# Inverse blocks transposed straight from the masked scores, key transposes moved into the inverse, token shift on VectorE, low-rank products on row halves

## The chip, the cores and the metric

One core of a Trainium2 chip runs one program. The metric is the device time of one execution in microseconds. Before: 2159.66 us, the median of three runs (2159.29 to 2162.8).

## The reference, cut to what matters

A sequence of 4096 tokens of width 1024 is normalised and modulated, multiplied with one input matrix, and goes through two branches: a pooling mixer (stage one of the kernel) and an RWKV-7 time mixing with 8 heads of size 64 (stage two). Both outputs are concatenated, multiplied with the output matrix, gated, added to the residual and normalised. The change touches only the RWKV part:

```python
seg = seg + (prev - seg) * mu_shift            # token shift: this row and the row before
r, w_lo, k, v, a_lo, z = jnp.split(seg, split_idx, axis=-1)
w_raw = w0 + jnp.tanh(w_lo) @ w_up             # low-rank decay, rank 64
a = jax.nn.sigmoid(a0 + a_lo @ a_up)           # low-rank rate, rank 64
...
def step(S, inp):                              # one token; S is (H, 64, 64)
    r_t, w_t, k_t, v_t, am_t, b_t = inp        # am = -kk, b = kk * a
    sa = jnp.einsum('bhij,bhj->bhi', S, am_t)
    S = S * w_t[:, :, None, :] + sa[..., None] * b_t[:, :, None, :] + v_t[..., None] * k_t[:, :, None, :]
    return S, jnp.einsum('bhij,bhj->bhi', S, r_t)
```

The kernel computes the recurrence in chunks of 64 tokens. Within a chunk it needs, for each head, the inverse of a 64x64 triangular matrix that is built from products of rates and keys.

## The kernel before, in words

**Stage one** (to about 420 us) normalises and transforms the input, runs the pooling branch, and writes the hidden rows in two float16 parts (hT_hi, hT_lo) to HBM. **Stage two** runs over 16 blocks `b` of 256 tokens (4 chunks, 8 heads, so 32 chunk-heads). In every block four things happen, and the last of them belongs to the next block:

- `scores(b)`: for each chunk the 64-row products of BK (keys) and AR (queries and rates) on TensorE into two PSUM banks (L673), masked by VectorE into `sc` (L680). Then, before, the four 128x128 transposes of this chunk's BK (`btp`, L701), copied by ScalarE to `BT` (L702). BT is first read in `chain` (L851).
- `inverse(b)`: the two 32x32 diagonal blocks of each of the 32 matrices are inverted. Before, ScalarE copies them from `sc` into a corner of `MT` (L719, twice), VectorE transposes the corner to `Ab` (L725) and scales it by `d2T` (L726), ScalarE copies `Ab` to the other 64 partitions (L727) and fills `W` from it (L729, twice). Then a loop of 30 steps, each of two dependent small VectorE operations (L735, L740). Behind it: a scale (L751), two transposes of W into MT (L753), one of MT into `MQ` (L754), a ScalarE copy (L755), and two rounds of 32x32 products (`qp` L764, `m21p` L772) with ScalarE copies between.
- `chain(b)`: the four chunks in turn, each with products that depend on the state S, evicted by ScalarE and VectorE.
- `front(b+1)`: a Python generator with the next block's 17 projections (`seg`, L558 to 571). A projection is 8 triplets of float16 matmuls (L563 to 565) into a PSUM tile with the tag "pj"; the pool has three such buffers, shared with the low-rank products `pl` (L596) and `pa` (L613), with `vps` (L638) and with `pb` (L651). ScalarE reads the tile twice, once for this row (L567) and once for the row before (`prev`, L569), and VectorE adds the two (L570).

The generator yields after every triplet. `fill(n)` advances it by n yields, so the constants FS, FI, FT, FQ, FA, FB, FY say how many triplets TensorE gets between the steps of scores, inverse and chain. In the last block `project` takes the place of the front. A scheduler then orders each engine's instructions; `tc.high_priority` lifts the steps of the inverse over the front's. On every engine instructions run in the order of its queue. In the low-rank products before, `up_w` and `up_a` are padded with zeros to 128 rows, so each product takes all 128 rows of `lo`, whose lower 64 partitions hold the decay's part and whose upper 64 the rate's.

Of the kernel before, what the change touches and what calls it, by code (L numbers as in the profile page):

```python
# [10 lines left out]
F32 = mybir.dt.float32  # L11
# [3 lines left out]
AF = mybir.ActivationFunctionType  # L15
ALU = mybir.AluOpType
# [4 lines left out]
P = 128  # L21
D = 1024
KT = D // P
NPAIR = 4
# [28 lines left out]
def kernel(  # L53
# [19 lines left out]
    TB2 = 256  # L73
    NB2 = T // TB2
    NCH = TB2 // C
    NI = NCH * NH

    FS, FT, FQ, FA, FB, FY = 2, 13, 4, 3, 2, 2
    FI = [5 - i % 2 for i in range(16)]
    PF = 0.6  # L80
    PRI = 400

    V, A, G, PE, SP = nc.vector, nc.scalar, nc.gpsimd, nc.tensor, nc.sync

    cpool = ctx.enter_context(tc.tile_pool(name="cpool", bufs=1))
# [17 lines left out]
    up_w, up_a = (cpool.tile([P, 512], F32, name=n) for n in ("up_w", "up_a"))  # L103
# [35 lines left out]
    with ExitStack() as ph:  # L139
# [313 lines left out]
        def prep_lora():  # L453
            for t_, o in ((up_w, 0), (up_a, 64)):
                G.memset(t_[64 - o : 128 - o], 0.0)
                SP.dma_start(t_[o : o + 64], lora_up[o : o + 64])

        NA = 3
        for b in range(NB1):
# [11 lines left out]
            if b == 0:  # L471
                prep_lora()
# [18 lines left out]
    with ExitStack() as ph:  # L491
# [56 lines left out]
        def front(b, f):  # L548
# [9 lines left out]
            def seg(m, name, bufs=2):  # L558
# [9 lines left out]
                pv_ = wk.tile([P, TB2], F32, tag="prev", name=f"prev{b}_{m}", bufs=2)  # L568
                A.activation(pv_, pp[:, :TB2], AF.Identity, bias=0.0, scale=c2[:, m : m + 1])  # L569
                V.tensor_add(sg, sg, pv_)  # L570
# [15 lines left out]
            for p in range(NPAIR):  # L586
# [7 lines left out]
                pl = ps_pj.tile([P, TB2], F32, tag="pj", name=f"pl{b}_{p}")  # L594
                ps_ = slice(p * P, (p + 1) * P)
                PE.matmul(pl, up_w[:, ps_], lo, start=True, stop=True)  # L596
                tw = wk.tile([P, TB2], F32, tag="tw", name=f"tw{b}_{p}")
                A.activation(tw, pl, AF.Tanh, bias=pv[:, HW0, p : p + 1], scale=0.5)
                A.activation(tw, tw, AF.Identity, bias=one, scale=1.0)
# [12 lines left out]
                pa = ps_pj.tile([P, TB2], F32, tag="pj", name=f"pa{b}_{p}")  # L612
                PE.matmul(pa, up_a[:, ps_], lo, start=True, stop=True)  # L613
                ta = wk.tile([P, TB2], F32, tag="ta", name=f"ta{b}_{p}")
                A.activation(ta, pa, AF.Tanh, bias=pv[:, HA0, p : p + 1], scale=0.5)
# [5 lines left out]
                V.tensor_mul(ta, ta, kS)  # L621
                V.tensor_mul(BK[:, p, :, 1, :], c3(ta), c3(Pi))
                V.tensor_mul(AR[:, p, :, 1, :], c3(rS), Pp[:, :, 1:])
# [36 lines left out]
        def scores(b, f, fill):  # L660
# [6 lines left out]
            for ch in range(NCH):  # L667
# [31 lines left out]
                pt = ps_sc.tile([P, 512], F32, tag="sc", name=f"btp{b}_{ch}")  # L699
                for p in range(NPAIR):  # L700
                    PE.transpose(pt[:, p * P : (p + 1) * P], BK[:, p, ch].rearrange("q a t -> q (a t)"), ident)  # L701
                A.copy(BT[:, ch, :], pt)  # L702
# [5 lines left out]
        def inverse(b, f, fill):  # L708
# [3 lines left out]
            fi = iter(FI)  # L712
            sc, d2T = f["sc"], f["d2T"]
            MT = f["UV"][0:64].rearrange("q c (h t) -> q (c h) t", h=NH)

            with tc.high_priority(offset=PRI):
                for kb in range(2):
                    o = 32 * kb
                    A.copy(MT[o : o + 32, :, 0:32], sc[o : o + 32, :, o : o + 32])  # L719
            fill(next(fi))  # L720
            Ab = blk.tile([P, 32, 32], F32, tag="Ab", name=f"Ab{b}")
            W = blk.tile([P, 16, 32], F32, tag="W", name=f"W{b}")

            with tc.high_priority(offset=PRI):
                V.transpose(Ab[0:64], MT[:, :, 0:32].rearrange("s i t -> s t i"))  # L725
                V.tensor_mul(Ab[0:64], Ab[0:64], d2T[0:64].unsqueeze(2).to_broadcast([64, 32, 32]))  # L726
                A.copy(Ab[64:128], Ab[0:64])  # L727
                for g in range(2):
                    A.copy(W[64 * g : 64 * g + 64], Ab[64 * g : 64 * g + 64].rearrange("q (t g) s -> q t g s", g=2)[:, :, g, :])  # L729
# [331 lines left out]
```

## Time and profile before

| | |
|---|---|
| median of three runs | 2159.66 us |
| the profiled execution's own time | 2165.94 us |
| its span | 2164.2 us |
| PE busy, share of the span | 2002.0 us, 93% |
| DVE busy | 1399.5 us, 65% |
| ACT busy | 1112.2 us, 51% |
| mean granted TensorE clock | 0.966 |

A busy PE in this profile is not a PE at its peak: matmuls are pipelined and their ends are modelled. How fast TensorE goes is read from the distance of the starts of successive matmuls, and where it waits from the idle time in brackets before an instruction. Stage two is periodic, so one block in the middle is read closely (block 8, from 889.74 us, and block 9 behind it, from 976.78 us).

### The profile page before, as it was taken

What the parts mean: (1) busy time and instruction counts of PE and PEld (TensorE: products, weight loads), DVE (VectorE), ACT (ScalarE), POOL (GpSimd) and SP (SyncE); (2) the same over time, 40 slices, a digit from 0 to 9 for tenths busy, and PEclk for the clock granted to TensorE, in tenths of its full rate; (3) what the DMA queues carried; (4) which work ended last, traced back from release to release, by engine and by line L of the source; (5) the groups of instructions that cost most, each with busy time, mean ns of one, the idle gap of its engine ahead of it and who ended that gap; (6) DMA issues with size and microseconds to landing.
All of it is one profiled execution on the core that took longest, in us unless ns stands there. A gap on an engine that the chain in (4) does not pass through costs nothing.

```text
span 2164.2 us, 48675 instructions
## 1 busy us (share of the span) xinstructions
PE 2002.0 (93%) x20186; PEld 1498.8 (69%) x20186; DVE 1399.5 (65%) x3501; ACT 1112.2 (51%) x2455; POOL 150.9 (7%) x272
## 2 busy tenths in 40 slices
PE   4999999998998998999989989999899889999998
PEld 2444444687777777777777777777777767788887
DVE  8798987456756767567566675675766857433433
ACT  2545433356566655666666656665666663321211
POOL 3000000000000000000000000000000000100000
PEclk7999999999999999999999999999999999999999
DMA  7876767200010110101001101011010433444431
GB/s 276 274 236 230 247 216 261 64 21 9 23 32 1 31 27 6 31 2 31 26 7 31 26 6 31 2 31 27 6 31 17 132 105 121 156 156 137 146 107 69
DMA packets 140463, 183.22 MB, mean 85 GB/s; under 512 B 12113, under 2 KB 94033, under 8 KB 140242
## 3 DMA queue, kind: packets, MB, share of 16 engines
q1 hardware_dynamic: 140242, 180.11, 25.4%
q8 instruction: 158, 2.59, 0.5%
q14 instruction: 63, 0.52, 0.1%
HBM read 121.22 MB, written 58.85 MB: 83 GB/s over the span
## 4 chain that ended last, share of the span: by engine, by line
PE 57%; DVE 23%; ACT 14%; issue 3%; DMA 2%; SPq 0%; POOL 0%; DVEq 0%; POOLq 0%; ACTq 0%
PE pj L563 6%; PE po L961 5%; PE po L963 5%; PE po L962 5%; PE pj L565 5%; PE pj L564 5%; PE pp L414 4%; PE pp L416 4%; PE pp L415 4%; DVE W L740 4%; DVE Wt L735 4%; PE scp_sc L673 2%; ACT mx L900 2%; PE psn L851 2%; ACT UV L719 1%
## 5 line engine op out<-in xcount | busy, mean ns | idle before, releaser
L563 PE MATMUL pj<-hh,w2h 128*128 128x257 f16 x2176 | 621.8, 286 | 57.2 <-ACT prev L569 54.7
L565 PE MATMUL pj<-hh,w2l 128*128 128x257 f16 x2176 | 615.3, 283 | 0.0
L564 PE MATMUL pj<-hl,w2h 128*128 128x257 f16 x2176 | 614.4, 282 | 0.0
L564 PEld LDWEIGHTS <-w2h 128*128 128x128 f16 x2176 | 221.5, 102 | 105.5 <-issue 72.2
L563 PEld LDWEIGHTS <-w2h 128*128 128x128 f16 x2176 | 218.9, 101 | 51.6
L565 PEld LDWEIGHTS <-w2l 128*128 128x128 f16 x2176 | 217.8, 100 | 38.4
L961 PE MATMUL po<-wo,mh 128*128 128x512 f32 x512 | 204.7, 400 | 5.5 <-ACT mh L945 5.5
L962 PE MATMUL po<-wo,mh 128*128 128x512 f32 x512 | 202.0, 395 | 0.0
L415 PE MATMUL pp<-lo,w1h 128*128 128x512 f16 x512 | 194.6, 380 | 1.2 <-DVE lo L227 1.2
L416 PE MATMUL pp<-hi,w1l 128*128 128x512 f16 x512 | 194.5, 380 | 0.0
L414 PE MATMUL pp<-hi,w1h 128*128 128x512 f16 x512 | 194.0, 381 | 0.4 <-ACT hi L226 0.2
L967 ACT ACTIVATE sq<-x 128x512 f32<-128x512 f32 x64 | 40.4, 631 | 214.7 <-DVE x L965 199.2
L965 DVE TENSOR_TENSOR x<-po,x 128x512 f32<-128x512 f32 x64 | 44.1, 689 | 156.5 <-PE po L963 156.5
L735 DVE TENSOR_TENSOR Wt<-W,Ab 128x30 f32<-128x30 f32 (+7 forms) x480 | 118.3, 247 | 37.7 <-ACT W L729 27.7
L569 ACT ACTIVATE prev<-pj,c 128x256 f32<-128x256 f32 x272 | 126.9, 467 | 0.0
L740 DVE TENSOR_TENSOR W<-W,Wt 128x30 f32<-128x30 f32 (+7 forms) x480 | 117.9, 246 | 9.1
L961 PEld LDWEIGHTS po<-wo,mh 128*128 128x128 f32 x512 | 96.9, 189 | 27.5 <-ACT mh L945 5.8
L962 PEld LDWEIGHTS po<-wo,mh 128*128 128x128 f32 x512 | 96.9, 189 | 22.2
L963 PE MATMUL po<-wo,ml 128*128 128x512 f32 x256 | 102.0, 399 | 0.0
L416 PEld LDWEIGHTS <-w1l 128*128 128x128 f16 x512 | 50.3, 98 | 61.8 <-issue 2.5
L414 PEld LDWEIGHTS <-w1h 128*128 128x128 f16 x512 | 50.3, 98 | 59.4 <-issue 1.5
L415 PEld LDWEIGHTS <-w1h 128*128 128x128 f16 x512 | 50.2, 98 | 59.2 <-issue 0.6
(248 smaller groups left out, 3850.9 us busy)
## 6 DMA issues: line engine op xcount, KB each, us to landing
x<-in_x_dram SPq DMA_DIRECT2D x64, 256.0 KB, 3.0
out_dram<-x SPq DMA_DIRECT2D x64, 256.0 KB, 2.1
xk<-in_xT_dram SPq DMA_DIRECT2D x56, 256.0 KB, 4.1
xt<-in_x_dram SPq DMA_DIRECT2D x28, 512.0 KB, 5.5
wada<-in_w_ada_dram SPq DMA_DIRECT2D x24, 512.0 KB, 7.0
w2raw<-in_w_in_dram SPq DMA_DIRECT2D x17, 512.0 KB, 5.5
hh<-hT_hi SPq DMA_DIRECT2D x32, 257.0 KB, 3.5
hl<-hT_lo SPq DMA_DIRECT2D x32, 257.0 KB, 3.0
```

Source lines behind the costliest of these rows:

```text
L414: PE.matmul(pp, w1_hi[m][:, k, :], hi, start=(k == 0), stop=False)
L415: PE.matmul(pp, w1_hi[m][:, k, :], lo, start=False, stop=False)
L416: PE.matmul(pp, w1_lo[m][:, k, :], hi, start=False, stop=(k == KT - 1))
L563: unpin(PE.matmul(pp, w2_hi[m][:, k, :], hh[k], start=(k == 0), stop=False))
L564: PE.matmul(pp, w2_hi[m][:, k, :], hl[k], start=False, stop=False)
L565: PE.matmul(pp, w2_lo[m][:, k, :], hh[k], start=False, stop=(k == KT - 1))
L569: A.activation(pv_, pp[:, :TB2], AF.Identity, bias=0.0, scale=c2[:, m : m + 1])
L735: V.tensor_mul(tmp[:, :n, :k], W[:, r0:, k : k + 1].to_broadcast([P, n, k]), Ab[:, k : k + 1, :k].to_broadcast([P, n, k]),)
L740: V.tensor_add(W[:, r0:, :k], W[:, r0:, :k], tmp[:, :n, :k])
L961: unpin(PE.matmul(po, mh[:, k, ts_], wo[0][k][n], start=(k == 0), stop=False))
L962: PE.matmul(po, mh[:, k, ts_], wo[1][k][n], start=False, stop=False)
L963: PE.matmul(po, (ml[:, k] if b % 2 == 0 else ml[k])[:, ts_], wo[0][k][n], start=False, stop=(k == KT - 1))
```

## The change

1. `inverse`: VectorE transposes the diagonal blocks straight from `sc` (two transposes of 32 partitions, L708 of the new file); the two ScalarE copies into MT are gone. W is filled by two VectorE copies (L712) in place of two by ScalarE.
2. The four groups of key transposes (`btp`) and their copies to BT go from `scores` to `inverse`, each followed by `fill(FE)` with FE = 2. FI becomes 4 everywhere (64 yields in place of 72), FT 12 in place of 13.
3. `up_w` and `up_a`, padded, become one tile `up`, loaded at the program's start; `pl` takes partitions 0 to 63, `pa` 64 to 127, and `pa` with its tanh moves up beside `pl`.
4. `seg`: the second ScalarE operation and the addition become one VectorE operation that reads the PSUM tile (L562 of the new file).

```diff
--- before.py
+++ after.py
@@ -75,8 +75,8 @@
     NCH = TB2 // C
     NI = NCH * NH
 
-    FS, FT, FQ, FA, FB, FY = 2, 13, 4, 3, 2, 2
-    FI = [5 - i % 2 for i in range(16)]
+    FS, FE, FT, FQ, FA, FB, FY = 2, 2, 12, 4, 3, 2, 2
+    FI = [4] * 16
     PF = 0.6
     PRI = 400
 
@@ -100,7 +100,8 @@
     SP.dma_start(vec, vecs)
 
 
-    up_w, up_a = (cpool.tile([P, 512], F32, name=n) for n in ("up_w", "up_a"))
+    up = cpool.tile([P, 512], F32, name="up")
+    SP.dma_start(up, lora_up)
 
     def pow2_scale(pool, psp, am, n, name):
 
@@ -450,11 +451,6 @@
             for f in todo[max(b - 1, 0) : b] if b < NB1 - 1 else todo[max(b - 1, 0) :]:
                 f()
 
-        def prep_lora():
-            for t_, o in ((up_w, 0), (up_a, 64)):
-                G.memset(t_[64 - o : 128 - o], 0.0)
-                SP.dma_start(t_[o : o + 64], lora_up[o : o + 64])
-
         NA = 3
         for b in range(NB1):
             if b == 0:
@@ -468,8 +464,6 @@
                 pz, pu = proj(b, hs, (4, 0))
                 pooled(b, 0, pu, gated(b, 0, pz))
             side(b)
-            if b == 0:
-                prep_lora()
             for g in range(1, 4):
                 if b == 0:
                     tz = tzs[g]
@@ -565,9 +559,7 @@
                     PE.matmul(pp, w2_lo[m][:, k, :], hh[k], start=False, stop=(k == KT - 1))
                 sg = wk.tile([P, TB2], F32, tag=name, name=f"{name}{b}_{m}", bufs=bufs)
                 A.activation(sg, pp[:, 1:], AF.Identity, bias=0.0, scale=c1[:, m : m + 1])
-                pv_ = wk.tile([P, TB2], F32, tag="prev", name=f"prev{b}_{m}", bufs=2)
-                A.activation(pv_, pp[:, :TB2], AF.Identity, bias=0.0, scale=c2[:, m : m + 1])
-                V.tensor_add(sg, sg, pv_)
+                V.scalar_tensor_tensor(sg, pp[:, :TB2], c2[:, m : m + 1], sg, op0=ALU.mult, op1=ALU.add)
                 return sg
 
             AR = blk.tile([P, NPAIR, NCH, 2, C], F32, tag="AR", name=f"AR{b}", bufs=2)
@@ -591,11 +583,14 @@
                 yield
                 rS = yield from seg(2 + 4 * p, "rS")
 
-                pl = ps_pj.tile([P, TB2], F32, tag="pj", name=f"pl{b}_{p}")
                 ps_ = slice(p * P, (p + 1) * P)
-                PE.matmul(pl, up_w[:, ps_], lo, start=True, stop=True)
+                pl, pa = (ps_pj.tile([P, TB2], F32, tag="pj", name=f"{n}{b}_{p}") for n in ("pl", "pa"))
+                PE.matmul(pl, up[0:64, ps_], lo[0:64], start=True, stop=True)
+                PE.matmul(pa, up[64:128, ps_], lo[64:128], start=True, stop=True)
                 tw = wk.tile([P, TB2], F32, tag="tw", name=f"tw{b}_{p}")
                 A.activation(tw, pl, AF.Tanh, bias=pv[:, HW0, p : p + 1], scale=0.5)
+                ta = wk.tile([P, TB2], F32, tag="ta", name=f"ta{b}_{p}")
+                A.activation(ta, pa, AF.Tanh, bias=pv[:, HA0, p : p + 1], scale=0.5)
                 A.activation(tw, tw, AF.Identity, bias=one, scale=1.0)
                 L = wk.tile([P, TB2], F32, tag="L", name=f"L{b}_{p}")
                 V.tensor_tensor_scan(L, rst, tw, 0.0, op0=ALU.mult, op1=ALU.add)
@@ -609,18 +604,14 @@
                 vS = yield from seg(3 + 4 * p, "vS")
                 if p == 0:
                     BK = f["BK"] = blk.tile([P, NPAIR, NCH, 2, C], F32, tag="BK", name=f"BK{b}")
-                pa = ps_pj.tile([P, TB2], F32, tag="pj", name=f"pa{b}_{p}")
-                PE.matmul(pa, up_a[:, ps_], lo, start=True, stop=True)
-                ta = wk.tile([P, TB2], F32, tag="ta", name=f"ta{b}_{p}")
-                A.activation(ta, pa, AF.Tanh, bias=pv[:, HA0, p : p + 1], scale=0.5)
                 tb = wk.tile([P, TB2], F32, tag="L", name=f"tb{b}_{p}")
                 V.scalar_tensor_tensor(tb, ta, 1.0, kS, op0=ALU.add, op1=ALU.mult)
                 A.activation(ta, ta, AF.Identity, bias=pv[:, OKA, p : p + 1], scale=pv[:, HKA, p : p + 1])
                 V.scalar_tensor_tensor(AR[:, p, :, 0, :], c3(kS), vec[:, V_KK + p : V_KK + p + 1], Pp[:, :, 0:C], op0=ALU.mult, op1=ALU.mult)
                 V.scalar_tensor_tensor(BK[:, p, :, 0, :], c3(tb), pv[:, NKK, p : p + 1], c3(Pi), op0=ALU.mult, op1=ALU.mult)
                 V.tensor_mul(ta, ta, kS)
+                V.tensor_mul(AR[:, p, :, 1, :], c3(rS), Pp[:, :, 1:])
                 V.tensor_mul(BK[:, p, :, 1, :], c3(ta), c3(Pi))
-                V.tensor_mul(AR[:, p, :, 1, :], c3(rS), Pp[:, :, 1:])
                 G.tensor_copy(pc[:, p, :], Pp[:, :, C])
                 if todo:
                     todo.pop(0)()
@@ -696,37 +687,37 @@
                         V.transpose(d2T[64 * g : 64 * g + 64], d2)
                 if ch in (0, 3):
                     f["todo"].pop(0)()
+                fill(FS)
+                if ch % 2 == 0:
+                    run(gns[0], 1)
+            f["sc"], f["BT"], f["d2T"] = sc, BT, d2T
+
+        def inverse(b, f, fill):
+
+
+
+            fi = iter(FI)
+            sc, d2T = f["sc"], f["d2T"]
+            MT = f["UV"][0:64].rearrange("q c (h t) -> q (c h) t", h=NH)
+
+            Ab = blk.tile([P, 32, 32], F32, tag="Ab", name=f"Ab{b}")
+            W = blk.tile([P, 16, 32], F32, tag="W", name=f"W{b}")
+            with tc.high_priority(offset=PRI):
+                for kb in range(2):
+                    o = 32 * kb
+                    V.transpose(Ab[o : o + 32], sc[o : o + 32, :, o : o + 32].rearrange("s i t -> s t i"))
+                V.tensor_mul(Ab[0:64], Ab[0:64], d2T[0:64].unsqueeze(2).to_broadcast([64, 32, 32]))
+                A.copy(Ab[64:128], Ab[0:64])
+                for g in range(2):
+                    V.tensor_copy(W[64 * g : 64 * g + 64], Ab[0:64].rearrange("q (t g) s -> q t g s", g=2)[:, :, g, :])
+            fill(next(fi))
+            BK, BT = f["BK"], f["BT"]
+            for ch in range(NCH):
                 pt = ps_sc.tile([P, 512], F32, tag="sc", name=f"btp{b}_{ch}")
                 for p in range(NPAIR):
                     PE.transpose(pt[:, p * P : (p + 1) * P], BK[:, p, ch].rearrange("q a t -> q (a t)"), ident)
                 A.copy(BT[:, ch, :], pt)
-                fill(FS)
-                if ch % 2 == 0:
-                    run(gns[0], 1)
-            f["sc"], f["BT"], f["d2T"] = sc, BT, d2T
-
-        def inverse(b, f, fill):
-
-
-
-            fi = iter(FI)
-            sc, d2T = f["sc"], f["d2T"]
-            MT = f["UV"][0:64].rearrange("q c (h t) -> q (c h) t", h=NH)
-
-            with tc.high_priority(offset=PRI):
-                for kb in range(2):
-                    o = 32 * kb
-                    A.copy(MT[o : o + 32, :, 0:32], sc[o : o + 32, :, o : o + 32])
-            fill(next(fi))
-            Ab = blk.tile([P, 32, 32], F32, tag="Ab", name=f"Ab{b}")
-            W = blk.tile([P, 16, 32], F32, tag="W", name=f"W{b}")
-
-            with tc.high_priority(offset=PRI):
-                V.transpose(Ab[0:64], MT[:, :, 0:32].rearrange("s i t -> s t i"))
-                V.tensor_mul(Ab[0:64], Ab[0:64], d2T[0:64].unsqueeze(2).to_broadcast([64, 32, 32]))
-                A.copy(Ab[64:128], Ab[0:64])
-                for g in range(2):
-                    A.copy(W[64 * g : 64 * g + 64], Ab[64 * g : 64 * g + 64].rearrange("q (t g) s -> q t g s", g=2)[:, :, g, :])
+                fill(FE)
             for k in range(30, 0, -1):
                 r0 = (k + 1) // 2
                 n = 16 - r0
```

What the scheduler makes of it is seen in the rows of the built program. First VectorE between the last masked scores of block 8 and the first step of the loop. `sc8` is the masked score tile, `kS9_1`, `rS9_2` are projections of the next block, `bon8` is the bonus term, whose operand `pb8_3` lies in a "pj" buffer. Before:

```order
L680 TENSOR_TENSOR sc8_14301<-scp8_3_px_14457,mask_3655 128x4x128
L570 TENSOR_TENSOR kS9_1_14471<-kS9_1_14471,prev9_1_14473 128x256
L652 TENSOR_TENSOR bon8_13079<-pb8_3_14485,vS8_15_14147 128x256
L725 STREAM_TRANSPOSE Ab8_14533<-UV8_13082 64x1024
L570 TENSOR_TENSOR rS9_2_14514<-rS9_2_14514,prev9_2_14516 128x256
L726 TENSOR_TENSOR Ab8_14533<-Ab8_14533,d2T8_14300 64x1024
L601 SCALAR_TENSOR_TENSOR L9_0_14524<-rst_3661,tw9_0_14521 128x256
L735 TENSOR_TENSOR Wt8_30_14540<-W8_14534,Ab8_14533 128x30
```

Now:

```order
L671 TENSOR_TENSOR sc8_13983<-scp8_3_px_14119,mask_3651 128x4x128
L562 SCALAR_TENSOR_TENSOR kS9_1_14133<-pj9_1_14062,c2_103,kS9_1_14133 128x256
L708 STREAM_TRANSPOSE Ab8_14154<-sc8_13983 32x1024 x2
L643 TENSOR_TENSOR bon8_12796<-pb8_3_14145,vS8_15_13872 128x256
L709 TENSOR_TENSOR Ab8_14154<-Ab8_14154,d2T8_13982 64x1024
L562 SCALAR_TENSOR_TENSOR rS9_2_14174<-pj9_2_14138,c2_103,rS9_2_14174 128x256
L712 COPY W8_14155<-Ab8_14154 64x512 x2
L596 SCALAR_TENSOR_TENSOR L9_0_14186<-rst_3657,tw9_0_14181 128x256
L726 TENSOR_TENSOR Wt8_30_14255<-W8_14155,Ab8_14154 128x30
```

The projections' operations now read PSUM (pj9_1, pj9_2); there is one transpose more and two copies more in the queue; `bon8` stands behind both transposes.

Second, VectorE at the end of the loop. Before:

```order
L735 TENSOR_TENSOR Wt8_1_14950<-W8_14534,Ab8_14533 128x15
L740 TENSOR_TENSOR W8_14534<-W8_14534,Wt8_1_14950 128x15
L570 TENSOR_TENSOR rS9_10_14911<-rS9_10_14911,prev9_10_14913 128x256
L751 TENSOR_TENSOR W8_14534<-W8_14534,d2T8_14300 128x512
L847 TENSOR_TENSOR Sd8_0_15187<-S_3682,pc8_13081 128x256
L753 STREAM_TRANSPOSE UV8_13082<-W8_14534 64x16x32 x2
L601 SCALAR_TENSOR_TENSOR L9_2_14921<-rst_3661,tw9_2_14918 128x256
L754 STREAM_TRANSPOSE MQ8_14953<-UV8_13082 32x1024
```

Now:

```order
L562 SCALAR_TENSOR_TENSOR kS9_9_14530<-pj9_9_14499,c2_103,kS9_9_14530 128x256
L726 TENSOR_TENSOR Wt8_2_14597<-W8_14155,Ab8_14154 128x15x2
L731 TENSOR_TENSOR W8_14155<-W8_14155,Wt8_2_14597 128x15x2
L726 TENSOR_TENSOR Wt8_1_14613<-W8_14155,Ab8_14154 128x15
L731 TENSOR_TENSOR W8_14155<-W8_14155,Wt8_1_14613 128x15
L742 TENSOR_TENSOR W8_14155<-W8_14155,d2T8_13982 128x512
L838 TENSOR_TENSOR Sd8_0_14832<-S_3678,pc8_12798 128x256
L744 STREAM_TRANSPOSE UV8_12799<-W8_14155 64x16x32 x2
L562 SCALAR_TENSOR_TENSOR rS9_10_14572<-pj9_10_14541,c2_103,rS9_10_14572 128x256
L745 STREAM_TRANSPOSE MQ8_14616<-UV8_12799 32x1024
```

The scan L9_2 is gone from between the transposes; the operation on `rS9_10`, the last reader of pj9_10, stands behind the transposes of W, where before it stood ahead of the scale.

Third, ScalarE at the same place (`tw9_2` and `ta9_2` are the tanh of the low-rank products, `UV9<-vps9_1` empties the PSUM tile of vps9_1). Before:

```order
L567 ACTIVATE rS9_10_14911<-pj9_10_14880,c1_102 128x256
L569 ACTIVATE prev9_10_14913<-pj9_10_14880,c2_103 128x256
L598 ACTIVATE tw9_2_14918<-pl9_2_14916,pv_3667 128x256
L644 COPY UV9_14327<-vps9_1_14926 64x2x128
L599 ACTIVATE tw9_2_14918<-tw9_2_14918,one_3680 128x256
L644 COPY UV9_14327<-vps9_1_14926 64x2x128
L755 COPY UV8_13082<-UV8_13082 32x32x32
L603 ACTIVATE Ppad0_3676<-L9_2_14921 128x4x64
L605 ACTIVATE Pi9_2_14924<-L9_2_14921 128x256
L567 ACTIVATE vS9_11_14976<-pj9_11_14937,c1_102 128x256
```

Now:

```order
L561 ACTIVATE rS9_10_14572<-pj9_10_14541,c1_102 128x256
L591 ACTIVATE tw9_2_14579<-pl9_2_14575,pv_3663 128x256
L593 ACTIVATE ta9_2_14581<-pa9_2_14576,pv_3663 128x256
L746 COPY UV8_12799<-UV8_12799 32x32x32
L594 ACTIVATE tw9_2_14579<-tw9_2_14579,one_3676 128x256
L635 COPY UV9_14009<-vps9_1_14589 64x2x128 x2
L598 ACTIVATE Ppad0_3672<-L9_2_14584 128x4x64
L600 ACTIVATE Pi9_2_14587<-L9_2_14584 128x256
L561 ACTIVATE vS9_11_14639<-pj9_11_14600,c1_102 128x256
```

The copy UV8<-UV8, which waits for VectorE's transposes of W, has moved ahead of the two copies that empty vps9_1. On TensorE the projection pj9_12 and the 8 products `px` of `lead` stand ahead of all 32 `qp8` products now; before, 13 of the 32 stood ahead of them.

## Rows read from the trace of the kernel before

**Rows 1.** Windows, two blocks, three stretches each: us, busy per engine, PEclk, DMA, GB/s.

```profile
889.74:904.77 15.03, 15.01 (x177) 12.39 (x176) 8.11 (x20) 7.57 (x19) 1.64 (x1) 1.00 0.27 73
904.77:944.23 39.46, 32.96 (x276) 27.97 (x274) 34.34 (x103) 24.95 (x55) 1.88 (x7) 0.99 0.03 7
944.23:976.78 32.55, 31.47 (x611) 24.22 (x611) 15.38 (x43) 21.64 (x57) 2.56 (x4) 0.91 0.04 10
...
991.83:1032.49 40.66, 34.59 (x276) 28.80 (x274) 34.40 (x103) 24.93 (x55) 1.87 (x7) 0.96 0.03 7
1032.49:1063.80 31.31, 30.24 (x612) 23.62 (x612) 15.38 (x43) 21.64 (x57) 2.56 (x4) 0.95 0.04 9
```

**Rows 2.** Waits of PE, whole span: us in total, times, longest.

```profile
PE pj L563 <- ACT prev L569: 54.7, 55, 2.3
PE qp L764 <- DVE MQ L754: 43.2, 15, 3.2
```

**Rows 3.** Windows behind four waits of PE, columns as above.

```profile
943.53:950.36 6.83, 6.13 (x53) 4.38 (x53) 4.08 (x10) 2.61 (x7) 1.33 (x2) 0.50 0.01 2
...
1032.28:1035.69 3.41, 3.20 (x39) 2.37 (x40) 3.19 (x10) 1.93 (x5) 0.84 (x2) 0.50 0.00 0
...
1004.97:1008.39 3.42, 3.42 (x19) 2.39 (x17) 3.42 (x14) 1.37 (x3) 0.00 (x0) 0.50 0.02 5
...
916.23:919.64 3.41, 2.38 (x22) 2.09 (x22) 3.38 (x14) 2.95 (x8) 0.44 (x1) 1.00 0.00 0
```

**Rows 4.** Timeline of PE, blocks 8 and 9: start, us, instruction, wait before it.

```profile
896.01 0.27 PE L565 MATMUL pj<-hh,w2l 128*128 128x257 f16 x1
896.22 0.37 PE L673 MATMUL scp_sc<-AR,BK 64*128 64x128 f32 x1
...
898.32 0.60 PE L701 MATMUL btp<-ident,BK 128*128 128x128 f32 x4
898.75 0.27 PE L563 MATMUL pj<-hh,w2h 128*128 128x257 f16 x1
...
899.09 0.28 PE L563 MATMUL pj<-hh,w2h 128*128 128x257 f16 x1
...
908.64 0.60 PE L596 MATMUL pl<-lo,up_w 128*128 128x256 f32 x2
...
917.26 0.27 PE L563 MATMUL pj<-hh,w2h 128*128 128x257 f16 x1 [2.27 <-ACT prev L569]
...
1004.28 0.27 PE L563 MATMUL pj<-hh,w2h 128*128 128x257 f16 x1 [2.25 <-ACT prev L569]
```

**Rows 5.** Timeline of DVE in block 8: the inverse's head and tail.

```profile
907.13 0.68 DVE L680 TENSOR_TENSOR sc<-scp_px,mask 128x512 f32<-128x512 f32 x1
...
909.98 1.96 DVE L725 STREAM_TRANSPOSE Ab<-UV 64x1024 f32<-64x1024 f32 x1 [1.50 <-ACT UV L719]
...
912.18 1.21 DVE L726 TENSOR_TENSOR Ab<-Ab,d2T 64x1024 f32<-64x1024 f32 x1
...
915.77 0.19 DVE L735 TENSOR_TENSOR Wt<-W,Ab 128x30 f32<-128x30 f32 x1 [1.79 <-ACT W L729]
...
938.87 0.19 DVE L740 TENSOR_TENSOR W<-W,Wt 128x15 f32<-128x15 f32 x1
...
942.97 1.21 DVE L754 STREAM_TRANSPOSE MQ<-UV 32x1024 f32<-32x1024 f32 x1
```

**Rows 6.** Groups by line, whole span: busy us, mean ns | idle before.

```profile
L569 ACT ACTIVATE prev<-pj,c 128x256 f32<-128x256 f32 x272 | 126.9, 467 | 0.0
...
L570 DVE TENSOR_TENSOR kS<-kS,prev 128x256 f32<-128x256 f32 x64 | 26.9, 420 | 90.9 <-ACT prev L569 90.9
...
L652 DVE TENSOR_TENSOR bon<-pb,vS 128x256 f32<-128x256 f32 x64 | 26.1, 407 | 0.0
...
L755 ACT COPY UV<-UV 32x1024 f32<-32x1024 f32 x16 | 16.7, 1044 | 46.7 <-DVE UV L753 46.7
```

**Rows 7.** The page's DMA issues: KB each, us to landing.

```profile
wada<-in_w_ada_dram SPq DMA_DIRECT2D x24, 512.0 KB, 7.0
```

More of the change, by code (lines that the diff above doesn't have):

```diff
@@ L698, in scores @@
                     f["todo"].pop(0)()
[L699 to L702, printed above, removed]
                 fill(FS)
@@ L728, in inverse @@
                 for g in range(2):
-                    A.copy(W[64 * g : 64 * g + 64], Ab[64 * g : 64 * g + 64].rearrange("q (t g) s -> q t g s", g=2)[:, :, g, :])
+                    V.tensor_copy(W[64 * g : 64 * g + 64], Ab[0:64].rearrange("q (t g) s -> q t g s", g=2)[:, :, g, :])
+            fill(next(fi))
+            BK, BT = f["BK"], f["BT"]
+            for ch in range(NCH):
+                pt = ps_sc.tile([P, 512], F32, tag="sc", name=f"btp{b}_{ch}")
+                for p in range(NPAIR):
+                    PE.transpose(pt[:, p * P : (p + 1) * P], BK[:, p, ch].rearrange("q a t -> q (a t)"), ident)
+                A.copy(BT[:, ch, :], pt)
+                fill(FE)
             for k in range(30, 0, -1):
```

## The prediction

> **What bounds the kernel now.** I read the windows of two neighbouring blocks first [rows 1]. A block takes 87.0 us (15.03 + 39.46 + 32.55), cut at its first score product, at S (the first triplet behind its last score products, 904.77) and at the first qp product; of the next block the last two stretches are shown, 40.66 and 31.31. In the first stretch TensorE is busy throughout. In the second VectorE is busy 34.3 us of 39.5 and TensorE only 33.0: there the inverse's chain on VectorE sets the end. In the third TensorE is busy again 31.5 of 32.6. The waits of PE then tell what stands at the border [rows 2]: 43.2 us in 15 waits of qp for MQ, some 2.9 us a block, and 54.7 us in 55 waits of a projection for ScalarE's `prev`, the last reader of its PSUM buffer, some 3.4 us a block. [...] Each block also has a wait of some 2.26 us for `prev` [rows 4]; behind that of block 9 the clock is 0.50 for another 3.42 us, behind that of block 8 it stays at 1.00 [rows 3]. Block 9's second stretch is 1.2 us longer, at a mean clock of 0.96 [rows 1].
>
> So a period is TensorE's work plus its waits plus what half clock costs. The rest of the program: stage one is not touched but for one DMA, and block 15 runs against `project`, whose products fill TensorE to the end.
>
> **Prices on TensorE** [rows 4]. A triplet is 0.33 us (898.75 to 899.09, rounded up there), a group of four transposes 0.43 (898.32 to 898.75); a low-rank product shows the same 0.60 as such a group, so 0.43 too.
>
> **Part by part, one period.** All times are from S.
>
> *Scores.* Three groups of transposes lie ahead of S; they go (-1.3), one triplet comes (+0.33, the constants give the rest of the block one more). TensorE sets the end there, so 15.03 becomes 14.05. The copies to BT go along; at nothing, since ScalarE is busy 25 us of 39.5 in the inverse [rows 1] and loses its copies and `prev` there. Were it full, each copy would hold a PSUM bank and with it the next transposes.
>
> *VectorE's head* [rows 5]. Before: the last masked score ends at S+3.04, the loop starts at S+11.0, and 1.50 + 1.79 us of that were waits for ScalarE's copies. Now those waits go, but work comes: a second transpose and two copies. The nearest row for a transpose of 1024 strided elements is L725, 1.96 us; the contiguous one, L754, took 1.21. The new source has twice L725's stride, so below 1.21 each, above 2.7 (the step from 1.21 to 1.96 paid again); I take 1.96. A copy of 512 elements has no row; the nearest is the scale, 1.21 for 1024, so 0.6, with bounds of half that and 0.68, the operation on sc. Then: kS9_1 to S+3.45, transposes to S+7.3, bon8 to S+7.65, scale to S+8.85, rS9_2 and the copies to S+10.4, scan to S+11.0. The loop starts where it started: what the copies by ScalarE cost, VectorE now pays itself.
>
> *The token shift.* `prev` goes from ScalarE, 17 x 0.47 us a block [rows 6], off the path. The VectorE operation gets a per-partition scalar and a PSUM operand; bon<-pb, which reads PSUM, takes 0.41 against 0.42 for the addition in SBUF [rows 6], so I charge 0.05 each, nine in the inverse, 0.4 us. [...]
> What weighs more is the wait: a "pj" buffer comes free only when VectorE, in its own queue behind the inverse, has read it. Loop 23.4 us (before 23.3 [rows 5]), then scale, Sd, transposes of W, rS9_10 and MQ without the scan between: MQ at S+38.9, 0.5 earlier than before.
>
> *TensorE in the inverse.* It has 89 triplets ahead of qp where it had 81 (pj9_12 comes ahead), three more groups of transposes, and the products of `lead`. Walking its queue against VectorE's:
> - 9 triplets, pb, pl9_0, five transposes, pa9_0: S+5.7. pj9_3 needs the buffer of pb8_3, whose reader bon8 ends at S+7.65 behind the transposes: 2.0 us wait.
> - Four projections with the other transposes: S+19.2. vps9_0 needs ScalarE's tanh of pl9_1 (two 0.47 operations behind): S+20.9, then pj9_7 needs rS9_6 on VectorE, S+22.5: 2.3 us wait in two pieces.
> - pj9_7 to pj9_10 with pb9_0: S+33.6; low-rank pair and vps9_1 with 0.8 of waits; pj9_11 from S+35.3 to S+37.95, pb9_1.
> - pj9_12 needs the buffer of vps9_1, emptied by ScalarE behind UV8<-UV8: transposes of W end S+37.3, copy 1.04, then three operations of at most 0.47 [rows 6]: S+39.7, 1.3 us wait. Then 2.65 and 0.45 for `lead`: qp at S+42.9, with MQ long there.
> The second stretch so grows from 39.46 to 42.9.
>
> *After qp.* Block 9 takes 31.31, of which 3.2 ran at half clock; without that 29.7. Nine triplets (-2.99) and `lead` (-0.45) have gone ahead; but without pj9_12 as cover behind the first qp, m21p waits for ScalarE's copies about 0.75 longer. 27.0.
>
> *Row halves.* pl and pa on different rows can run side by side, as the two score products do. But the first score product starts 0.21 behind a projection matmul where 0.11 is usual [rows 4], so each change of shape costs about 0.1. Two pairs a block that stand together (p = 1, 3) save 0.44 - 0.2 each, the pair split by transposes (p = 0) pays 0.4, p = 2 waits between. Sum 0.
>
> [...]
>
> *Start.* One load of 256 KB now stands ahead of the first weights; 512 KB take 7.0 us to land [rows 7], so 0 to 3.5; +1, since queues overlap. Block 0's front ran without an inverse beside it and block 15 is filled by `project`: 0, within 3 each.
>
> **Sum.** 14.05 + 42.9 + 27.0 = 83.95 against 87.04, without half clock. Some comes back: the 2.0 and 2.3 us waits are as long as the two of which one was followed by half clock [rows 3]. A stretch of 3.41 us costs up to 1.7 us; the first has slack behind it (TensorE waits there anyway), the second has none. I charge 0.8: 84.75, so 2.3 less. Fourteen periods (blocks 1 to 14), 32 us, less 1 for the start: 31 off the profiled execution's 2165.94, which makes 2135. The median lies 6.3 under that execution, so 2129 us.
>
> **Rivals.**
> - *Waits without half clock, or cheap transposes* (chance 0.27): half clock stays away (-0.8 more), or the transposes take nearer 1.21 (-1.5 in head, bon8 and all behind). Together 4.6 a period, 64 us: 2095. For: block 8's wait of 2.27 us brought none. Against: block 9's of 2.25 did.
> - *Handed back* (0.07): VectorE and TensorE wait for each other at every buffer, each semaphore costing some 0.1 us more than my walk, 2 us a period: 2155 to 2164.
> - *Slower* (0.14): the two waits each bring a stretch as long as block 8's 6.83 us at half clock, in which TensorE sets the pace: 3.4 us lost twice, against 3.1 won. +3.7 a period, 52 us: 2211; with transposes at 2.7 as well, 2230. It decides from 3.1 us lost a period. For: the buffer now waits on the busiest engine of the stretch. Against: rows 3 show such a length only where the wait for MQ was followed by tiny qp products.
> - *It does not do what it says*: if ScalarE, relieved of 8 us, was the real brake of the whole second stretch, all 3.4 us of `prev` waits would go and MQ decide at S+38.9: period 80, 2061. Chance 0.01, since the built order puts VectorE's readers behind the transposes.
>
> **Numbers.** The forecast itself has 0.51. A measurement tells about 0.2%, 4 us, from no change. Faster: 0.51 + 0.27 + 0.01 = 0.79; same 0.07; slower 0.14. The range leaves out the slower case and the deep end of the faster: 2094 to 2163.
>
> **What would show it.** Right: periods near 84.8 us between first score products; PE waits of pj for bon and for rS (VectorE), no long wait of qp for MQ; the loop's first step still near S+11; score stretch 14.0 us; pb to pj9_3 idle near 2 us. Wrong: a transposing row far from 1.96; granted clock below 0.90 over a whole period; or waits at pj9_12 and vps9_1 above 3 us.

## The result, and the profile after

The changed kernel takes 2129.45 us (median of four runs, 2129.28 to 2131.77) against 2161.23 us before on the same chip: ratio 0.9849, interval 0.9836 to 0.9862, so faster by 1.5%. 2129 was forecast. The profiled execution took 2131.77 us, its span is 2130.1 us.

One correction to the text ahead: the blocks called 8 and 9 there are, counted from 0, numbers 5 and 6. The program is periodic, so only the names of tiles are touched; "pj9_12" below is the thirteenth projection of the next block, whatever the block. The rows of after are those of its block 8, from 1135.24 us to 1220.07 us; S is 1149.16.

Windows of this block, its three stretches and the half-clock piece in the second (us, then busy time of PE, PEld, DVE, ACT, POOL, then PEclk, the mean granted clock, and the share and GB/s of DMA):

```profile
1135.24:1149.16 13.92, 13.92 (x168) 11.35 (x168) 8.22 (x20) 5.20 (x14) 1.64 (x1) 1.00 0.34 91
1149.16:1193.19 44.03, 39.72 (x327) 32.19 (x325) 40.65 (x114) 21.61 (x47) 2.48 (x8) 0.96 0.02 7
1193.19:1220.07 26.88, 25.28 (x573) 19.27 (x569) 12.51 (x36) 18.25 (x48) 1.93 (x2) 1.00 0.03 6
1157.23:1160.64 3.41, 3.41 (x18) 2.65 (x16) 3.04 (x8) 1.44 (x2) 0.25 (x2) 0.50 0.02 5
```

Against [rows 1], the first stretch lost 1.1 us, the second grew by 3.4 to 4.6, the third lost 4.4 to 5.7: work moved ahead of qp. VectorE is now busy 40.65 us of 44.03 there, where it had 34.3 of 39.5. The waits of PE show what went (us in total, times, longest):

```profile
PE vps L629 <- ACT tw L591: 25.7, 47, 0.6
PE pj L557 <- DVE bon L643: 23.9, 14, 1.7
...
PE pj L557 <- DVE rS L562: 12.5, 15, 1.2
PE pj L557 <- ACT UV L635: 12.0, 14, 1.2
...
PE qp L755 <- DVE MQ L745: 2.9, 1, 2.9
```

Against [rows 2], the 15 waits of qp for MQ have become one, that of block 0, and those for `prev` are gone; four smaller ones came, none above 1.7 us. VectorE's timeline at the inverse's head, to hold against [rows 5]:

```profile
1152.52 3.87 DVE L708 STREAM_TRANSPOSE Ab<-sc 32x1024 f32<-32x1024 f32 x2
1156.42 0.42 DVE L643 TENSOR_TENSOR bon<-pb,vS 128x256 f32<-128x256 f32 x1
1156.76 1.21 DVE L709 TENSOR_TENSOR Ab<-Ab,d2T 64x1024 f32<-64x1024 f32 x1
1157.89 0.47 DVE L562 SCALAR_TENSOR_TENSOR rS<-pj,c,rS 128x256 f32<-128x256 f32 x1
1158.29 0.84 DVE L712 COPY W<-Ab 64x512 f32<-64x512 f32 x2
...
1159.77 0.16 DVE L726 TENSOR_TENSOR Wt<-W,Ab 128x30 f32<-128x30 f32 x1
...
1161.18 0.48 DVE L610 SCALAR_TENSOR_TENSOR AR<-kS,vec,Ppad 128x256 f32<-128x256 f32 x1 [0.80 <-ACT Ppad L598]
```

And TensorE's, where bon holds up pj9_3, and where pj9_12 now stands ahead of qp:

```profile
1156.90 0.27 PE L557 MATMUL pj<-hh,w2h 128*128 128x257 f16 x1 [1.71 <-DVE bon L643]
...
1188.10 0.60 PE L642 MATMUL pb<-rk,bones 128*128 128x256 f32 x2
1189.83 0.27 PE L557 MATMUL pj<-hh,w2h 128*128 128x257 f16 x1 [1.13 <-ACT UV L635]
1192.58 0.68 PE L789 MATMUL px<-UV,sc 64*64 64x64 f32 x16
1193.19 0.75 PE L755 MATMUL qp<-MQ,sc 32*32 32x32 f32 x64
```

### The profile page after: what moved, and what is told of

Same layout as the page of the kernel before. It is cut to its first block, busy times and chain, and to the rows that moved or that the text cites. A ratio compares the mean times of both kernels' runs of the same rounds, so it can differ in the third digit from the quotient of the medians.

```text
span 2130.1 us, 48341 instructions
## 1 busy us (share of the span) xinstructions
PE 1984.4 (93%) x20186; PEld 1464.5 (69%) x20186; DVE 1454.7 (68%) x3549; ACT 966.0 (45%) x2119; POOL 148.3 (7%) x270
## 4 chain that ended last, share of the span: by engine, by line
PE 54%; DVE 28%; ACT 10%; issue 4%; DMA 2%; POOL 0%; SPq 0%; DVEq 0%; ACTq 0%; POOLq 0%
PE po L952 6%; PE po L954 5%; PE po L953 5%; PE pj L557 5%; DVE W L731 4%; PE pj L559 4%; PE pj L558 4%; DVE Wt L726 4%; PE pp L415 4%; PE pp L416 4%; PE pp L417 4%; DVE Ab L708 3%; PE psn L826 2%; PE scp_sc L664 2%; PE px L814 2%
## 5 line engine op out<-in xcount | busy, mean ns | idle before, releaser
L557 PE MATMUL pj<-hh,w2h 128*128 128x257 f16 x2176 | 609.4, 280 | 49.8 <-DVE bon L643 23.9
L559 PE MATMUL pj<-hh,w2l 128*128 128x257 f16 x2176 | 603.9, 278 | 0.0
L558 PE MATMUL pj<-hl,w2h 128*128 128x257 f16 x2176 | 601.9, 277 | 0.0
L558 PEld LDWEIGHTS <-w2h 128*128 128x128 f16 x2176 | 217.5, 100 | 89.0 <-issue 59.1
L557 PEld LDWEIGHTS <-w2h 128*128 128x128 f16 x2176 | 214.8, 99 | 52.2 <-issue 6.5
L559 PEld LDWEIGHTS <-w2l 128*128 128x128 f16 x2176 | 213.4, 98 | 34.0
L953 PEld LDWEIGHTS po<-wo,mh 128*128 128x128 f32 x512 | 96.6, 189 | 22.3
L562 DVE SCALAR_TENSOR_TENSOR kS<-pj,c,kS 128x256 f32<-128x256 f32 x64 | 30.6, 478 | 101.5 <-ACT kS L561 101.5
```

The lines of the kernel that those rows point to most:

```text
L557: unpin(PE.matmul(pp, w2_hi[m][:, k, :], hh[k], start=(k == 0), stop=False))
L558: PE.matmul(pp, w2_hi[m][:, k, :], hl[k], start=False, stop=False)
L559: PE.matmul(pp, w2_lo[m][:, k, :], hh[k], start=False, stop=(k == KT - 1))
L953: PE.matmul(po, mh[:, k, ts_], wo[1][k][n], start=False, stop=False)
```

## The experiments

**One part undone, one part alone.** Four kernels are the changed one with one part taken back, four the kernel before with one part alone. The parts are shown cut to a line or two each, before and changed. Not shown: the keys' part also moves the btp products and BT copies from scores to inverse; the head's also fills W by VectorE; the rows' also allocates pa's tile beside pl's, takes pa's product and tanh ahead, swaps two VectorE products and loads `up` at the program's start.

```diff
@@ keys
-    FS, FT, FQ, FA, FB, FY = 2, 13, 4, 3, 2, 2
-    FI = [5 - i % 2 for i in range(16)]
+    FS, FE, FT, FQ, FA, FB, FY = 2, 2, 12, 4, 3, 2, 2
+    FI = [4] * 16
@@ shift
-                A.activation(pv_, pp[:, :TB2], AF.Identity, bias=0.0, scale=c2[:, m : m + 1])
-                V.tensor_add(sg, sg, pv_)
+                V.scalar_tensor_tensor(sg, pp[:, :TB2], c2[:, m : m + 1], sg, op0=ALU.mult, op1=ALU.add)
@@ head
-                    A.copy(MT[o : o + 32, :, 0:32], sc[o : o + 32, :, o : o + 32])
+                    V.transpose(Ab[o : o + 32], sc[o : o + 32, :, o : o + 32].rearrange("s i t -> s t i"))
@@ rows
-                PE.matmul(pl, up_w[:, ps_], lo, start=True, stop=True)
+                PE.matmul(pl, up[0:64, ps_], lo[0:64], start=True, stop=True)
+                PE.matmul(pa, up[64:128, ps_], lo[64:128], start=True, stop=True)
```

Expected without the keys' part, without the shift, without the head, without the row halves:

> The changed kernel with one part undone: the keys' transposes stand in the scores again, with the old fill constants. My theory: the gain comes from TensorE work (three groups of transposes, 1.3 us, and nine triplets of the thirteenth segment, 2.99 us) standing where TensorE had waited some 2.9 us a block for MQ and then run at half clock. Then this kernel keeps the wait of qp for MQ (some 2.5 to 3 us a block) and is 0 to 10 us faster than the kernel before, where the whole change gave 31.8. Rival one (the relief of ScalarE by the token shift is the gain) and rival two (the staging copies' removal is the gain): 25 to 35 us faster, as with the whole change.

> The changed kernel with one part undone: the token shift's second term goes through ScalarE's prev copy again. My theory: ScalarE is not on the path, and its copies only release the buffers a little later; the wait of a projection for the shift's sum on VectorE gives way to one for prev. 26 to 36 us faster than the kernel before, so within 5 us of the whole change. Rival one (relief of ScalarE is the gain): 0 to 10 us faster than before, waits of pj for prev of 3 us a block or more.

> The changed kernel with one part undone: the inverse's blocks are staged by ScalarE again (copies to MT and to W), one contiguous transpose on VectorE. My theory: the loop starts at S+11.0 instead of S+10.6 and MQ ends 0.4 us later, which TensorE, some 4 us behind MQ in the changed kernel, does not notice; the product behind the first low-rank term comes sooner, because bon of the block before is no longer behind 3.9 us of transposes (its wait of 1.7 us shrinks to 0 to 1). 28 to 45 us faster than before, that is 0 to 13 faster than the whole change. Rival two (the removed staging is the gain): 0 to 10 us faster than before.

> The changed kernel with one part undone: the two low-rank products are padded to all rows again and stand where they stood. My theory: two products side by side save 0.3 us a pair at two places and pay as much at change of shape; 28 to 36 us faster than before, within 4 us of the whole change. Rival three (the pairs' overlap is a gain of 0.43 us each, 1.7 a block): 8 to 16 us faster than before.

Expected with one part alone:

> The kernel before with one part of the change alone: keys' transposes in the inverse, with the new fill constants. My theory: the 2.9 us wait of qp for MQ is filled by TensorE work, and with it goes one of the two stretches of 3.41 us at half clock a block; 15 to 35 us faster than the kernel before, no long wait of qp for MQ. Rivals one and two (relief of ScalarE, removed staging): 0, or slower by up to 10, since ScalarE gets eight more copies inside the inverse.

> The kernel before with one part alone: the token shift's second term by VectorE from PSUM. My theory: the waits of a projection for prev become waits for VectorE, MQ still sets the end, and VectorE's queue gets some 0.06 us longer for each of nine operations in the inverse: from 8 us faster to 8 us slower. Rival one (relief of ScalarE is the gain): 20 to 32 us faster.

> The kernel before with one part alone: blocks transposed without staging. My theory: VectorE's own transposes and copies cost about what the waits for ScalarE cost; the loop starts 0.4 us sooner at most, MQ 0.4 us sooner in 15 blocks: 0 to 8 us faster. Rival two (removed staging is the gain, 3.3 us of waits a block): 20 to 35 us faster.

> The kernel before with one part alone: row halves for the low-rank products. My theory: MQ sets the end, so what TensorE saves in the inverse is waited out: within 4 us of the kernel before. Rival three (overlap of the pairs, 1.7 us a block): 16 to 24 us faster.

Measured, these and the four runs below. "Less" is the median of the kernel before on the same chip minus this one's. Period, idle and half clock are per block, means over blocks 1 to 14 of the profiled execution: idle is the window less PE's busy time in it, half clock the time that the clock's records show at 0.50.

| kernel | ratio to before | less, us | period | idle | half clock |
|---|---|---|---|---|---|
| before | 1 | 0 | 87.23 | 7.36 | 7.31 |
| the whole change | 0.9849 [0.9836, 0.9862] | 31.8 | 84.85 | 6.12 | 2.93 |
| without keys | 0.9835 [0.9822, 0.9848] | 36.3 | 84.72 | 6.63 | 2.68 |
| without shift | 1.0018 [1.0010, 1.0027] | -3.8 | 87.79 | 7.41 | 8.29 |
| without head | 0.9786 [0.9772, 0.9799] | 47.2 | 84.23 | 6.04 | 3.17 |
| without rows | 0.9901 [0.9887, 0.9914] | 22.3 | 85.63 | 6.66 | 0.73 |
| keys alone | 0.9952 [0.9934, 0.9971] | 10.7 | 86.28 | 7.15 | 2.93 |
| shift alone | 0.9883 [0.9867, 0.9898] | 25.6 | 85.27 | 6.20 | 5.61 |
| head alone | 0.9900 [0.9883, 0.9918] | 21.3 | 85.61 | 8.33 | 0.24 |
| rows alone | 0.9793 [0.9778, 0.9807] | 44.7 | 84.14 | 6.55 | 3.41 |
| before, qp held back | 0.9967 [0.9955, 0.9979] | 5.8 | 86.70 | 7.74 | 6.10 |
| without shift, qp held back | 1.0058 [1.0046, 1.0070] | -12.7 | 88.27 | 7.97 | 6.83 |
| bon early | 0.9873 [0.9861, 0.9886] | 26.6 | 85.37 | 5.10 | 6.10 |
| head as before, FT 8, FQ 8 | 0.9631 [0.9618, 0.9643] | 79.8 | 81.86 | 4.65 | 1.95 |

The windows from which the idle times come, of before and of after:

```profile
540.45:1761.67 1221.22, 1118.21 (x14842) 907.36 (x14841) 810.38 (x2310) 758.37 (x1793) 84.92 (x154) 0.96 0.10 27
```

```profile
542.73:1730.57 1187.84, 1102.12 (x14842) 876.65 (x14841) 860.09 (x2352) 630.13 (x1499) 84.74 (x154) 0.98 0.10 28
```

(1221.22 - 1118.21) / 14 is 7.36, and so on. My theory by parts fell: none of these eight runs came out in the range that was expected for it. The keys' transposes, to which I gave the gain, can be taken back at no loss. The row halves, to which I gave nothing, are worth 44.7 us alone. The shift, "off the path", is the one part without which nothing is gained. The head costs some 13 to 15 us in company. Of the rivals, two were met: that ScalarE's relief is the gain (the shift alone, 20 to 32 us) and that the removed copies are (the head alone, 20 to 35 us); but with all parts together the second fails, since without the head the kernel is faster.

The four parts alone add up to 102 us, the whole is 32, so they are not four separate savings. In all four kernels with one part alone the wait of some 3 us for MQ is gone from block 1 on. What comes in its place differs: with the head alone TensorE idles 1 us a block more than before, and the gain goes with the half clock, 0.24 us a block where it was 7.31; with the rows alone both idle time and half clock fall. The waits of PE in the kernel with the rows alone, and in the one without the shift:

```profile
PE vps L631 <- ACT prev L563: 42.4, 45, 1.7
PE pj L557 <- ACT prev L563: 32.0, 30, 1.8
...
PE m21p L765 <- ACT MQ L759: 8.6, 14, 0.6
```

```profile
PE qp L757 <- DVE MQ L747: 57.3, 15, 4.9
PE vps L631 <- ACT prev L563: 38.4, 31, 2.4
```

**Is it the order on TensorE?** In the kernel before, the built order (the order that the scheduler gave TensorE's queue) has 13 qp products ahead of pj9_12; in the changed one, and in those with the shift or the rows alone, pj9_12 is ahead of all of them. So I held qp back by an edge to the instruction ahead of it, in the kernel before and in the one without the shift:

```diff
-                    PE.matmul(pt[32 * q : 32 * q + 32, j * 32 : (j + 1) * 32], sc[0:32, i, 32:64], MQ[0:32, i, :], start=True, stop=True)
+                    tc.keep_in_program_order(PE.matmul(pt[32 * q : 32 * q + 32, j * 32 : (j + 1) * 32], sc[0:32, i, 32:64], MQ[0:32, i, :], start=True, stop=True))
```

> The kernel before with its TensorE order changed and nothing else: the 32 qp products are held behind what stands ahead of them in the text, so all 8 triplets of the thirteenth projection (2.65 us), one more triplet and the lead products go ahead of qp, where 13 qp products stood ahead of them. New theory after the first eight runs (each part alone was 11 to 45 us faster, 102 together, the whole 32): what all parts have in common is that the built order puts that projection ahead of qp, which fills TensorE's wait of 3.0 us a block for MQ and takes one of two stretches of 3.41 us at half clock a block away. Then this kernel is 18 to 40 us faster than before, with no long wait of qp for MQ, waits for prev still there. Rival (each part saves what it saves by itself, by its own operations): within 6 us of before, the wait going to m21p or prev instead.

> The changed kernel without the token shift's part, as in the run that came out 4 us slower than before, with the qp products held behind what stands ahead of them in the text; there 9 of them stood ahead of vps, a whole projection segment and another one, 5.7 us of work, and 3.84 us a block were lost in the wait for MQ. New theory: the token shift's part matters only by where the planner then puts qp; held in place, this kernel is 20 to 40 us faster than before. Rival (moving the shift to VectorE is itself needed, since ScalarE is the brake): from 6 us slower to 8 us faster than before.

The theory of the order fell: the first is 5.8 us faster than before where 18 to 40 were expected, the second 12.7 slower where 20 to 40 faster were. TensorE's and VectorE's timelines of the kernel before with qp held back show why:

```profile
1282.10 0.59 PE L651 MATMUL pb<-rk,bones 128*128 128x256 f32 x2
1285.99 0.38 PE L563 MATMUL pj<-hh,w2h 128*128 128x257 f16 x1 [3.30 <-DVE bon L652]
```

```profile
1281.70 2.08 DVE L753 STREAM_TRANSPOSE UV<-W 64x512 f32<-64x512 f32 x2
1283.82 0.69 DVE L601 TENSOR_TENSOR_SCAN L<-rst,tw 128x256 f32<-128x256 f32 x1
1284.42 1.21 DVE L754 STREAM_TRANSPOSE MQ<-UV 32x1024 f32<-32x1024 f32 x1
1285.57 0.37 DVE L652 TENSOR_TENSOR bon<-pb,vS 128x256 f32<-128x256 f32 x1
```

pj9_12 could not have run earlier. Its "pj" buffer is that of pb9_1, and what empties it is bon9_1, which stands on VectorE right behind MQ. The 3.0 us for MQ became 3.30 us for bon: one wait with two claimants, of which the profile of before could only name the first in TensorE's queue. In the kernel without the shift, with qp held back, it is vps9_1 that waits. It has the buffer of pj9_10, whose last reader, a `prev`, stands on ScalarE behind the copy that itself waits for VectorE's transposes of W (ScalarE's timeline, then TensorE's; 2.7 to 4.9 us a block, 4.4 in the mean, where the wait for MQ had 3.8):

```profile
1298.09 1.04 ACT L748 COPY UV<-UV 32x1024 f32<-32x1024 f32 x1 [1.14 <-DVE UV L746]
1299.15 0.47 ACT L563 ACTIVATE prev<-pj,c 128x256 f32<-128x256 f32 x1
```

```profile
1299.68 0.71 PE L631 MATMUL vps<-cmat,vS 128*128 128x128 f32 x4 [2.73 <-ACT prev L563]
```

So the theory that the runs leave: **one of TensorE's three "pj" buffers hung on a reader queued behind the end of the inverse's chain.** The built programs agree. Of the fourteen, only the kernel before and the same with qp held back give pj9_12 the buffer of pb9_1 (in 14 of 15 blocks), so that it needs bon9_1. In the kernel with the rows alone it has the buffer of vps9_1, which ScalarE empties ahead of its copy that waits for VectorE (no wait); in the changed one too, but there the emptying stands behind that copy (1.13 us). With the shift alone it has that of pa9_2, released by a tanh (1.1 us of wait at most). With the keys or the head alone it has that of pj9_11, and TensorE, which comes there later against the end of MQ, meets waits of 1.1 to 1.4 us for the UV copies and for `prev` in place of one of 3.0. The three buffers do not go round in a fixed turn: before, pb9_1 and pj9_12 follow each other in the same one, and the assignment changed also with parts that move no "pj" allocation.

This was argued from the runs after they were known. That moving bon9_1 alone ahead of MQ would give the same was not tried, nor was allocating pa beside pl without the other things that the rows' part does.

**The wait for bon.** In the changed kernel bon8 stands behind 3.87 us of strided transposes, and pj9_3 waits 1.71 us for it. One edit brings it ahead of them:

```diff
-                if ch in (0, 3):
+                if ch in (0, 2):
                     f["todo"].pop(0)()
```

> The changed kernel with pb8_3's product and its reader bon one chunk earlier in the scores, so that bon stands ahead of the strided transposes in VectorE's queue. Theory: what the unstaged blocks cost (without them the kernel was 15 us faster) is the wait of a projection for bon, 1.7 us a block, and the split of a low-rank pair; about half of it turns up in the next wait, for rS on VectorE's queue: 38 to 48 us faster than before, the whole change having 32. Rival one (all of the wait moves to the next reader): 28 to 36 faster. Rival two (each us of that wait counts in full): 54 or more faster.

A miss on the wrong side: 26.6 us less than before, where the change gave 31.8 (the two intervals just meet). The idle time fell by 1.0 us a block, as expected, but the half clock doubled, from 2.93 to 6.10 us a block. TensorE's timeline has three waits close together, and the window that begins with the second has the clock at 0.50 for 6.83 us:

```profile
1172.25 0.70 PE L589 MATMUL pa<-lo,up 64*128 64x256 f32 x2 [1.18 <-DVE kS L562]
1173.52 1.22 PE L629 MATMUL vps<-cmat,vS 128*128 128x128 f32 x4 [0.57 <-ACT tw L591]
1175.39 0.37 PE L557 MATMUL pj<-hh,w2h 128*128 128x257 f16 x1 [0.65 <-DVE rS L562]
```

```profile
1172.90:1179.73 6.83, 5.61 (x26) 4.00 (x26) 6.40 (x22) 3.38 (x9) 0.19 (x1) 0.50 0.00 0
```

**A version that beats both.** In the changed kernel without the head, qp comes 1 to 2 us behind MQ, and m21p then waits 1.82 us a block, four waits together, for the copies of qp (the list counts the first of each four, the others are below 0.15):

```profile
PE m21p L766 <- ACT MQ L760: 19.3, 14, 1.7
```

In that kernel four triplets are moved from ahead of qp to behind it:

```diff
-    FS, FE, FT, FQ, FA, FB, FY = 2, 2, 12, 4, 3, 2, 2
+    FS, FE, FT, FQ, FA, FB, FY = 2, 2, 8, 8, 3, 2, 2
```

> Three parts of the change (keys' transposes, row halves, token shift), the staging copies kept, and 4 triplets moved from ahead of qp to behind it (FT 8, FQ 8 for 12 and 4). In the run with these three parts qp stands 1 to 2 us behind MQ's end, and m21p then waits 1.8 us a block for ScalarE's copies of qp, behind 4 triplets (1.3 us). Theory: the 4 moved triplets cover most of that wait, 0.8 to 1.4 us a block: 56 to 68 us faster than before. Rival (the triplets were needed as cover for MQ, which qp then waits for, or half clock follows): 36 to 48 us faster, no better than without the move.

2083.01 us, 79.8 less than before, 3.7%, and more than expected. The waits of m21p are gone; what is left on PE in stage two are waits of at most 1.1 us:

```profile
PE vps L629 <- ACT tw L591: 26.4, 48, 0.6
...
PE pj L557 <- DVE rS L562: 15.5, 15, 1.1
PE pj L557 <- ACT tw L591: 13.9, 15, 1.0
```

Its windows for a block without half clock: the second stretch is 4.2 us shorter than in the changed kernel's block 8 (which has a stretch of it), the third only 0.6 longer.

```profile
1108.47:1122.41 13.94, 13.94 (x168) 11.35 (x168) 8.27 (x20) 5.22 (x14) 1.64 (x1) 1.00 0.34 93
1122.41:1162.20 39.79, 36.27 (x316) 30.09 (x314) 34.62 (x102) 22.45 (x49) 1.88 (x7) 1.00 0.03 7
1162.20:1189.70 27.50, 26.17 (x581) 20.22 (x581) 15.59 (x44) 19.64 (x51) 2.90 (x4) 1.00 0.03 6
```

Of the 2.37 us that the move brings a period against the kernel without the head (84.23 to 81.86), 1.39 are idle time and, by estimate, some 0.6 half clock (half of 1.22). The keys and the shift may not be needed here: the rows alone gave 44.7 us where the three parts gave 47.2, with intervals that overlap, and the rows alone with these two constants were not tried.

## Why the prediction was right, and where its reasons were not

*The sum.* Forecast 84.75 a period, with 0.8 for half clock; block 8 has 84.83. Blocks 1, 7 and 12, whose clock stays at 1.00, have 84.02 to 84.07, forecast 83.95; by stretches 13.92, 43.2 to 43.3 and 26.9, forecast 14.05, 42.9 and 27.0. Fourteen periods give 33.4 us (1221.22 less 1187.84) for 32. The rest nearly cancels: +1.1 to the first score product, +1.2 in block 0, which still waits for MQ, -3.1 behind the start of block 15. The +1 for the start is not shown: the seven other kernels with the same load came to the first score product 0.3 to 2.0 us earlier than the kernel before. That loads overlap at the start is shown: the first 10 us of the kernel before move 263 GB/s, where 512 KB in 7.0 us alone are 75. That the median fell within a microsecond of 2129 is luck on top: the profiled execution came out 3 us below its forecast of 2135, and it lies 2.3 us above its median where 6.3 were taken over from before.

*TensorE in the inverse.* Walked out right, almost wait by wait: 2.0 for bon8 (1.71), 1.3 at pj9_12 for the UV copy (1.13), 0.8 at the second pair (0.56), MQ long there at qp. Two pieces of 2.3 came out smaller (0.56 and 0.35), MQ a us later, at S+39.9.

*Prices.* The strided transpose took 1.93 (1.96). The copy of W took 0.42 for the 0.6 I chose, as long for its 512 elements as bon for 256 in the rows above. The shift's operation takes 0.47 from PSUM, the 0.42 and 0.05 that were charged, and L610, of the same form but from SBUF, 0.48 in the rows above: the operand in PSUM shows no extra cost here. The loop starts at S+10.6 (11.0), but its second step then meets a wait of 0.80 for ScalarE's Ppad that I had not seen.

*Half clock.* The clock's records, 54 before and 34 after, have 1.00 or 0.50 and nothing between. 0.8 a period was charged, 0.8 it is in the mean (84.85 less the 84.04 of the blocks without half clock). Against the kernel before, a period is 2.38 us shorter: 1.24 of idle time and, by estimate, 1.96 of half clock (half of the busy time at 0.50, 6.85 less 2.93), with 0.81 more of products at full clock on the other side, which I cannot split further.

*The steps that failed.* The total was right, but three steps give the parts a worth that the runs deny. "Row halves. ... Sum 0" holds for the products themselves (start to start, without waits, pl and pa take 3.4 us of TensorE a block for 3.5; where they stand together they do run side by side, from 1170.15 and 1170.16, and the change of shape shows as 0.20 behind the start of the projection matmul before them where 0.11 is usual), but I counted operations and not buffers: the part alone is worth 44.7 us. The likely reason is the other buffer of pj9_12; which of the things that the part does brings it was not separated. "`prev` goes from ScalarE, off the path" failed likewise: without the shift's part 9 qp products stand ahead of vps9_1 and wait 3.84 us a block for MQ, vps9_1 itself waits behind ScalarE's copy once they are held back, and the whole gain is gone. "What the copies by ScalarE cost, VectorE now pays itself" was right for the loop's start and wrong as a balance: alone the part gains 21.3 us, in company it costs 13 to 15, of which 4.9 are block 0, whose qp goes back behind MQ. That "pj9_12 comes ahead" I read from the built order without asking why it had stood behind. The answer was to be had then: beside qp's wait for MQ, which buffer the next projection takes, and who empties it.

The rival of slower, long half-clock stretches behind the new waits, did not come in this kernel; in bon early such stretches of 6.83 us came, and the gain got smaller. The 0.1 us a semaphore in *Handed back* was a guess of mine; no run shows it.

## What to carry to other kernels

A wait in a profile has one name, that of the first instruction in the queue (here 3.0 us for MQ, and 3.30 for bon once qp was held back); before an edit is priced by it, ask of the next two or three instructions what they wait for. With few buffers, here three, a change elsewhere can decide which buffer a later tile gets and so which reader it waits for (here pj9_12: 3.30 us, 1.13 or none); see that no such reader stands behind the end of a long chain in its queue. Parts that each remove the same wait do not add up (102 us one by one, 31.8 together), so a bundle should be taken apart: here three parts with two constants moved are worth 79.8 us, all four parts with the constants as they were 31.8.

## What was not expected of the hardware

How long TensorE idled did not tell how long the clock was halved. With the head alone it idles 8.33 us a block, the most of all fourteen kernels, mostly in seven waits of 0.5 to 1.5 us that begin 2 to 10 us apart, and the 14 blocks have one stretch at 0.50. Before, with 7.36 us, two waits of 2.3 and 3.0 us among them, there are 22. In the kernel with bon early three waits of 2.4 us together, inside 5 us, came with 6.83 us at 0.50 from the second wait on. So the sum of the idle time does not order these kernels; they differ in how it lies, and that this is the reason is not shown. The same pattern of waits (0.57 and 1.09 us) was followed by 3.41 us at 0.50 in block 9 of the fastest kernel and not in block 8; why was not settled.
